# Two units' scores in one interruption, and a bias table whose transfer is issued later

## The chip, the cores and the metric

The kernel runs on one NeuronCore of a Trainium2 chip. The metric is the device time of one execution in microseconds (us). Its engines are TensorE (PE in the profile, with PEld for its weight loads), VectorE (DVE), ScalarE (ACT), GpSimd (POOL) and SyncE (SP), which only issues transfers here. Each engine works through its own instructions in order; semaphores tie the engines together.

## The reference, cut to what matters

One layer of a streaming encoder: 256 rows of a new stream and 64 rows of a running one, 320 columns in all once they are transposed. The input is normalised and projected by one matrix into queries, keys, values and the two halves of a gated branch; attention over a band of chunks, with a relative-position bias and a sink for each head, runs beside that gated branch; both are projected back, and a feed-forward block follows.

```
def sink_attention(q, k, v, bias, sinks, valid=None):
    s = jnp.einsum('...qhgd,...khd->...hgqk', q, k).astype(jnp.float32) * (HEAD_DIM ** -0.5) + bias
    ...
    m = jnp.maximum(jnp.max(s, axis=-1), sink)
    p = jnp.exp(s - m[..., None])
    w = p / (jnp.sum(p, axis=-1, keepdims=True) + jnp.exp(sink - m)[..., None])
    return jnp.einsum('...hgqk,...khd->...qhgd', w.astype(v.dtype), v)

def reference(...):
    q, k, v, zs = project(xp, ln_mix_g[l], w_in[l], q_norm_g[l], k_norm_g[l])
    a_o = attn_prompt(q, k, v, rel_bias_table, attn_sinks[l])
    u, sv = sgu_inputs(zs, sgu_norm_g[l])
    s_o = sgu_prompt(u, sv, sgu_w[l], sgu_b[l])
    ...
    xp = finish(xp, a_o, s_o, out_norm_attn_g[l], out_norm_sgu_g[l], w_out[l],
                ln_ffn_g[l], w_ffn_up[l], w_ffn_down[l])
```

`rel_bias_table` has 32 buckets for each of 16 heads; the bias of a head depends only on the distance between query and key, so one row of 255 values per head holds it all.

## The kernel before, in words

Everything is held transposed, features on the 128 partitions and the 320 rows of both streams along the free axis. Each product is made of three: activations and weights are split into a high part (ScalarE, L116 for weights, L212 for x) and the rest (VectorE, L117 and L213), and TensorE multiplies high by high, high by low and low by high into the same accumulator.

**The first products.** x comes in tiles of 128 features (`xT`, 16 of them; two at a time from the ninth on). As each tile lands, the loop of L223 to L252 splits it, splits the matching rows of the weights for the first quarter of the queries (`q0_ps`) and for keys and values (`kv_ps`), and multiplies. Sums of squares of x are gathered beside it (L295, L297, L299).

**The stream of weights.** After that, `products` (L123) works through the rest of W_in in column groups of 256: q1, q2, q3, then four groups of v and four of u. Each group is four pieces; a piece is one load of 512 KB (`w_raw`), its two halves, and 24 products. `load` (L106) puts these loads on SyncE's queue, each behind the one before it, and takes up to four further transfers from the list `between` along with each: first the cached values, then the 16 reads of the bias (L280), then other constants. So SyncE's queue is weights, then up to four of the list, then weights.

**Interruptions.** With `between_pieces`, small work is put behind a given piece: the mean of the squares of x behind the first piece of q1 (L193, L194, on operands from L180 and L181), key norms, transposes of the values, and the attention by `attend`. TensorE's order is thus written out by hand; `issue_after` places an instruction behind another. The remaining order on the engines comes from a scheduler.

**Attention.** There are eight units: for each of the two key/value heads, query blocks 0 and 1 together, then 2, 3 and 4. `attend(i)` does, in one interruption, the transposes of the probabilities of unit i-2, the scores of unit i (L438) into the two score banks, and the weighted sums of unit i-3 (L520); behind these stands the softmax of unit i on VectorE, ScalarE and GpSimd. The transposes go to a pair of `misc` banks (there are two of these), the scores to `score_bank` (one for each half). attend(0) stands behind the second piece of q3, attend(1) behind its fourth; from the first v group on there are two per group.

**The bias.** GpSimd issues the transfer of the table (L86, `tab`, 16 x 32 values, transposed on the way) while the first tiles of x are loading. After the eighth tile in the program's order it builds the row of 255 values for each head by 29 copies from `tab` (L250) and writes it to DRAM, repeated 15 times (`b_dram`, L252). The 16 reads of `between` fetch it back from there in shifted rows, so that each partition has its own distances (`bias`), and the softmax adds it (L460).

Of the kernel before, what the change touches and what calls it, by code (L numbers as in the profile page):

```python
# [31 lines left out]
def hymba_step_kernel(ctx: ExitStack, tc: tile.TileContext, i, o):  # L32
    nc = tc.nc
# [12 lines left out]
    def misc():  # L46
        return ps_m.tile([P, 512], F32, name="misc", tag="misc")
# [7 lines left out]
    def blk(name, shape, dt=F32):  # L55
        return actp.tile(shape, dt, name=name, tag="B", bufs=6)
# [3 lines left out]
    xT = const.tile([P, KT, T], F32, name="xT")  # L60
# [5 lines left out]
    tab = const.tile([16, 32], F32, name="tab")  # L66
# [16 lines left out]
    for _ in range(4):  # L83
        nc.tensor.matmul(out=warm_ps[:, 0:256], lhsT=nc.const_aps.tensor(0.0, [P, P], F32),
                         rhs=nc.const_aps.tensor(0.0, [P, 256], F32), start=True, stop=True)
    nc.gpsimd.dma_start(out=tab, in_=i["table"].rearrange("b h -> h b"))  # L86
    inv_1k = const.tile([P, 1], F32, name="inv_1k")
    nc.vector.memset(inv_1k, 1.0 / 1024)

# [14 lines left out]
    firsts, loads, between, rests, steps, narrow, carry = [], [], [], [], [], [], []  # L104

    def load(out, in_):  # L106


        for o_, i_ in [(out, in_)] + [between.pop(0) for _ in range(min(4, len(between)))]:
            with tc.issue_after(loads[-1].ins) if loads else nullcontext():  # L110
                loads.append(nc.sync.dma_start(out=o_, in_=i_))  # L111
# [111 lines left out]
    for a, n in [(a, 1) for a in range(8)] + [(a, 2) for a in range(8, KT, 2)]:  # L223
        if a and a % 4 == 0:
            ahead = blk("w_first", [P, 2, 4, 256])
        raw = ahead[:, :, a % 4:a % 4 + n]
        load(xT[:, a:a + n], xv[:, a:a + n])
        for k in range(n if a > 1 else 0):
            load(raw[:, :, k], wv[:, a + k, 0:2048].rearrange("p (j c) -> p j c", j=2)[:, :, 0:256])
        for k in range(a, a + n):  # L230
            split(xT[:, k], g_mix[:, k:k + 1], XH[:, k], XL[:, k], pinned=True)
        hi, lo = [t.rearrange("p (j k) c -> p j k c", j=2)[:, :, 0:n] for t in w_tiles()]
        if a > 1:
            high, low = halves(raw, hi, lo, pinned=True)
        else:
            for j in range(2):
                if a or not j:
                    load(raw[:, j, 0], wv[:, a, j * 1024:j * 1024 + 256])
                high, low = halves(raw[:, j, 0], hi[:, j, 0], lo[:, j, 0], pinned=True)

        for x, (w_, r_) in enumerate(((hi, xh), (hi, xl), (lo, xh))):
            for j, k, g in [(j, k, g) for j in range(2) for k in range(n) for g in range(2)]:
                ps = q0_ps[g] if j == 0 else kv_ps[:, g]
                mm = nc.tensor.matmul(out=ps[:, 0:T], lhsT=w_[:, j, k, g * P:(g + 1) * P], rhs=r_(a + k),  # L244
                                      start=(a + k == 0 and x == 0), stop=(a + k == KT - 1 and x == 2))
        steps.append((high, low, mm.ins))
        if a == 7:
            b_row = sm.tile([16, 255], F32, name="b_row", tag="w1", bufs=3)
            for b, m, n in bucket_runs():
                nc.gpsimd.tensor_copy(out=b_row[:, m:m + n], in_=tab[:, b:b + 1].to_broadcast([16, n]))  # L250
            b_dram = dram.tile([16, 15, 255], F32, name="b_dram")
            nc.gpsimd.dma_start(out=b_dram, in_=b_row[:, None, :].to_broadcast([16, 15, 255]))  # L252
# [133 lines left out]
    def keys():  # L386
        for dst, c in ((kn[:, 0:256], slice(0, 256)), (kn[:, 384:448], slice(256, 320))):
            nc.vector.scalar_tensor_tensor(out=dst, in0=zk[:, c], scalar=g_k, in1=rk[:, c], op0=ALU.mult, op1=ALU.mult)
        for h in range(2):
# [10 lines left out]
                    between_pieces={0: first_norms, 1: lambda: (values(), norm_q(0, (q0_sq, q1_sq[0])), values_out()), 2: keys},  # L400
                    halves_behind={1: lambda: (q0_out, *parts_k[2:4])})
    q2_sq = evict_q(2, q2_ps)
# [18 lines left out]
            yield (w, n0, kv) + blocks[b]  # L421
            n0 += len(blocks[b][4])

    probs, ready, maxed = {}, [], []
    room = blk("vnat", [P, 2560])
    vnat = room[:, 0:2048].rearrange("p (t c) -> p t c", t=2)

# [4 lines left out]
    def scores(u, s_ps):  # L432
        for w, n0, kv, q0, k0, nk, _, _ in parts(u):
            for j in range(2):
                a = 2 * (2 * kv + j)
                for x, p in [(x, p) for x in range(2) for p in range(2)]:
                    hs = slice(p * HD, (p + 1) * HD)
                    mm = nc.tensor.matmul(out=s_ps[p][x * HD:(x + 1) * HD, n0 * P + j * nk:n0 * P + (j + 1) * nk],  # L438
                                          lhsT=qT[hs, q0 // HD, a + x], rhs=kz[hs, kv, k0:k0 + nk], start=True, stop=True)
        return mm  # L440
# [45 lines left out]
    def attend(i, beside=None):  # L486

        n = len(groups)
        turns = [t for t in ((i - 2,), (n - 2, n - 1), ())[max(0, i - n + 1)] if t >= 0]
        outputs = [v for v in ((i - 3,), (i - 3,), (n - 2, n - 1))[max(0, i - n + 1)] if v >= 0]  # L490
        pairs = [[misc(), misc()]] if turns else []
        if i < n or len(turns) > 1 or beside:
            pairs.append([score_bank(p) for p in range(2)])
        s_ps = pairs[-1] if i < n else None
        places = [(pairs[0], 384), (pairs[-1], 384) if len(pairs) > 1 else (pairs[0], 256)]
        hs = [slice(r * HD, (r + 1) * HD) for r in range(2)]

        def behind(mms):
            with tc.issue_after(narrow[-1]):
                narrow.append([mm() for mm in mms][-1].ins)  # L500

        def turn(t, bank):
            s = probs.pop(t)
            behind([lambda p=p, n=n, x=x: nc.tensor.transpose(  # L504
                        out=bank[x][:, (p * 3 + n) * HD:(p * 3 + n + 1) * HD],
                        in_=s[hs[x], p, n].rearrange("x j k -> x (j k)"), identity=ident[hs[x], hs[x]])
                    for p in range(2) for n in range(3) for x in range(2)])

        for t, bank in zip(turns, pairs):
            turn(t, bank)  # L510
        if s_ps:
            behind([lambda: scores(i, s_ps)])
        if beside:
            with tc.issue_after(narrow[-1]):
                outs = beside(pairs[0])
        sides = [(v, [b[:, c:c + P] for b in bank]) + part
                 for (v, part), (bank, c) in zip(((v, part) for v in outputs for part in parts(v)), places)]
        if sides:
            behind([lambda v=v, side=side, n0=n0, n=n, x=x, kv=kv, ts=ts, j=j, p=p:
                    nc.tensor.matmul(out=side[j][hs[p]], lhsT=vz[hs[j], x, kv], rhs=pts[v % 2][hs[j], :, p, n0 + n],  # L520
                                     start=n == 0, stop=n == len(ts) - 1)
                    for v, side, _, n0, kv, _, _, _, _, ts in sides for n, x in enumerate(ts) for j in range(2) for p in range(2)])
        if s_ps:
            softmax(i, s_ps)
        for _, side, _, _, kv, q0, *_ in sides:
            for j in range(2):
                nc.scalar.activation(out=ao[:, 4 * kv + 2 * j:4 * kv + 2 * j + 2, q0:q0 + 64],
                                     in_=side[j].rearrange("p (a q) -> p a q", a=2), func=AF.Copy)
        for t, bank in zip(turns, pairs):
            for x in range(2):  # L530
                with tc.issue_after(maxed[0]) if t and s_ps else nullcontext():
                    nc.vector.tensor_copy(out=pts[t % 2][:, x],
                                          in_=bank[x][:, 0:384].rearrange("k (p n q) -> k p n q", p=2, n=3))

        if beside:
            for out in outs:
                out()

    q3_ps = product(w_in, 0, KT, 768, xh, xl,
                    between_pieces={1: lambda: attend(0), 3: lambda: attend(1)})  # L540
    q3_sq = evict_q(3, q3_ps)

    def add_square(acc, src, first):
        if first:
# [22 lines left out]
    gvs = room[:, 2048:2560].rearrange("p (a t) -> p a t", a=8)  # L567
    for g in range(4):
        v_ps = product(w_in, 0, KT, 2304 + g * 256, xh, xl, between_pieces={
            1: lambda: (attend(2 * g + 2), norm_q(1, (q2_sq, q3_sq)) if g == 0 else None), 3: lambda: attend(2 * g + 3)} if g < 3 else {  # L570
            2: lambda: attend(8)})
        gelu2(v_ps, gv[:, 2 * g:2 * g + 2], maxed[0])
        for a in range(2 * g, 2 * g + 2):
            add_square(acc_v, gv[:, a], a == 0)
        for a in ((), (), range(6), range(6, 8))[g]:
            for dst, c in ((gv[:, a, 0:256], slice(0, 256)), (gvs[:, a], slice(256, T))):
                with tc.issue_after(ready[0]):
                    nc.gpsimd.tensor_scalar(out=dst, in0=gv[:, a, c], scalar1=g_sv[:, a:a + 1], scalar2=None, op0=ALU.mult)
# [225 lines left out]
```

## Time and profile before

| | us |
|---|---|
| median of 3 runs (1235.59 to 1235.89) | 1235.69 |
| the profiled execution | 1235.83 |
| its span, first to last instruction | 1234.0 |
| TensorE busy in it | 1229.5 |
| VectorE busy | 656.8 |
| ScalarE busy | 492.7 |
| GpSimd busy | 109.9 |

A line of the profile names the kernel's line (L...), the engine, the operation, output <- inputs by tile, the shape and a count. In a timeline the first two numbers are start and length in us; what stands in brackets is the engine's idle time before it and what ended that. `q` behind an engine's name is its queue: an instruction that issues or waits. In a table of windows stand the stretch, its length, busy time and count for each engine, then TensorE's granted clock as a share, the DMA engines' busy share and what they moved in GB/s. fp32 matmuls appear as two instructions each.

### The profile page before, as it was taken

To read this page: it belongs to the slowest core of one execution; us is meant where nothing else is said; L and a number is where in the kernel's file an instruction comes from. 1 tells how busy PE (TensorE), PEld (TensorE's weight loads), DVE (VectorE), ACT (ScalarE), POOL (GpSimd) and SP (SyncE) were. 2 spreads that over 40 slices of the span, in tenths; PEclk is the share of its full clock that TensorE was granted. 3 is DMA by queue.
4 is the path that set the end of the run, shared out by engine and by line. 5 is a ranking of instruction groups with operands and counts; after the bars stand their busy time and mean duration, and the time that the engine had idled before them with its cause. 6 is when DMAs were issued, how large, how long until landed. Compare 5 with 4: busy or idle time off the path is not lost.

```text
span 1234.0 us, 20673 instructions
## 1 busy us (share of the span) xinstructions
PE 1229.5 (100%) x8723; PEld 1222.0 (99%) x8723; DVE 656.8 (53%) x741; ACT 492.7 (40%) x655; POOL 109.9 (9%) x141
## 2 busy tenths in 40 slices
PE   9999999999999999999999999999999999999998
PEld 9999999999999999999999999999999999999998
DVE  7868868877864444344444443444444444444343
ACT  7446565435544433323443233333432234433321
POOL 3144653002200000000000000000000000000000
PEclk9999999999999999999999999999999999999999
DMA  9753456444554444445544444444444454445540
GB/s 284 225 146 107 120 144 190 154 144 147 154 153 146 148 150 154 151 144 150 154 153 145 146 154 153 145 148 152 154 149 145 151 154 149 145 151 164 175 159 32
DMA packets 187917, 188.02 MB, mean 152 GB/s; under 512 B 7600, under 2 KB 187360, under 8 KB 187824
## 3 DMA queue, kind: packets, MB, share of 16 engines
q1 hardware_dynamic: 186528, 185.48, 48.5%
q0 software_dynamic: 864, 0.98, 0.4%
q8 instruction: 68, 1.11, 0.4%
q10 hardware_dynamic: 432, 0.24, 0.1%
q14 instruction: 25, 0.20, 0.0%
HBM read 183.10 MB, written 3.35 MB: 151 GB/s over the span
## 4 chain that ended last, share of the span: by engine, by line
PE 99%; DMA 0%; ACT 0%; SPq 0%; DVE 0%; issue 0%; DVEq 0%
PE acc L144 94%; PE misc L144 1%; PE q_ps L244 1%; PE acc L244 1%; PE s_ps L438 1%; DMA xT<-in_xT 0%; PE misc L504 0%; PE misc L520 0%; PE s_ps L520 0%; PE misc L618 0%; PE g_ps L618 0%; PE misc L334 0%; PE misc L606 0%; SPq L111 0%; PE misc L194 0%; PE misc L193 0%
## 5 line engine op out<-in xcount | busy, mean ns | idle before, releaser
L117 DVE TENSOR_TENSOR w_lo<-w_raw,w_hi 128x1024 fp32r<-128x1024 f32 x332 | 417.2, 1257 | 437.0 <-ACT w_hi L116 427.8
L116 ACT ACTIVATE w_hi<-w_raw 128x1024 fp32r<-128x1024 f32 x332 | 351.8, 1060 | 672.0 <-PE acc L144 646.9
L144 PE MATMUL acc<-H2H,w_lo 128*128 128x320 f32 x1024 | 316.4, 309 | 0.0
L144 PE MATMUL acc<-H2H,w_hi 128*128 128x320 f32 x1024 | 316.4, 309 | 0.0
L144 PE MATMUL acc<-H2L,w_hi 128*128 128x320 f32 x1024 | 316.4, 309 | 0.0
L144 PE MATMUL acc<-FH,w_hi 128*128 128x320 f32 x992 | 306.5, 309 | 0.0
L144 PE MATMUL acc<-FL,w_hi 128*128 128x320 f32 x992 | 306.5, 309 | 0.0
L144 PE MATMUL acc<-FH,w_lo 128*128 128x320 f32 x992 | 306.5, 309 | 0.0
L144 PEld LDWEIGHTS acc<-H2H,w_hi 128*128 128x128 f32 x1024 | 192.2, 188 | 0.0
L144 PEld LDWEIGHTS acc<-H2L,w_hi 128*128 128x128 f32 x1024 | 192.2, 188 | 0.0
L144 PEld LDWEIGHTS acc<-H2H,w_lo 128*128 128x128 f32 x1024 | 192.2, 188 | 0.0
L144 PEld LDWEIGHTS acc<-FH,w_hi 128*128 128x128 f32 x992 | 186.2, 188 | 0.0
L144 PEld LDWEIGHTS acc<-FL,w_hi 128*128 128x128 f32 x992 | 186.2, 188 | 0.0
L144 PEld LDWEIGHTS acc<-FH,w_lo 128*128 128x128 f32 x992 | 186.2, 188 | 0.0
L144 PE MATMUL acc<-XH,w_hi 128*128 128x320 f32 x352 | 110.3, 313 | 0.0
L144 PE MATMUL acc<-XH,w_lo 128*128 128x320 f32 x352 | 108.8, 309 | 0.0
L144 PE MATMUL acc<-XL,w_hi 128*128 128x320 f32 x352 | 108.7, 309 | 0.0
L144 PEld LDWEIGHTS acc<-XH,w_hi 128*128 128x128 f32 x352 | 66.1, 188 | 2.7 <-issue 2.3
L144 PEld LDWEIGHTS acc<-XL,w_hi 128*128 128x128 f32 x352 | 66.1, 188 | 0.0
L144 PEld LDWEIGHTS acc<-XH,w_lo 128*128 128x128 f32 x352 | 66.1, 188 | 0.0
L712 DVE SCALAR_TENSOR_TENSOR tf<-acc,r 128x640 f32<-128x640 f32 x32 | 26.4, 825 | 41.8 <-PE acc L144 41.8
L727 DVE TENSOR_TENSOR xT<-xT,acc 128x640 f32<-128x640 f32 x31 | 25.5, 822 | 41.8 <-PE acc L144 41.8
(216 smaller groups left out, 1039.1 us busy)
## 6 DMA issues: line engine op xcount, KB each, us to landing
w_raw<-in_w_up SPq DMA_DIRECT2D x128, 512.0 KB
w_raw<-in_w_down SPq DMA_DIRECT2D x128, 512.0 KB
w_raw<-in_w_in SPq DMA_DIRECT2D x44, 512.0 KB
w_raw<-in_w_out SPq DMA_DIRECT2D x32, 512.0 KB
w_first<-in_w_in SPq DMA_DIRECT2D x14, 256.0 KB
out_yT<-xT SPq DMA_DIRECT2D x7, 320.0 KB
xT<-in_xT SPq DMA_DIRECT2D x8, 160.0 KB
xT<-in_xT SPq DMA_DIRECT2D x4, 320.0 KB
```

The lines of the kernel that those rows point to most:

```text
L116: return (pin(nc.scalar.activation(out=hi, in_=raw, func=AF.Copy)).ins, pin(nc.vector.tensor_tensor(out=lo, in0=raw, in1=hi.bitcast(F32), ...
L117: pin(nc.vector.tensor_tensor(out=lo, in0=raw, in1=hi.bitcast(F32), op=ALU.subtract)).ins)
L144: mm = nc.tensor.matmul(out=out, lhsT=w_[:, k, g * P:(g + 1) * P], rhs=r_(kk), start=(kk == 0 and x == 0), stop=(kk == nk - 1 and x == 2))
L244: mm = nc.tensor.matmul(out=ps[:, 0:T], lhsT=w_[:, j, k, g * P:(g + 1) * P], rhs=r_(a + k), start=(a + k == 0 and x == 0), stop=(a + k == ...
L438: mm = nc.tensor.matmul(out=s_ps[p][x * HD:(x + 1) * HD, n0 * P + j * nk:n0 * P + (j + 1) * nk], lhsT=qT[hs, q0 // HD, a + x], rhs=kz[hs, ...
L712: nc.vector.scalar_tensor_tensor(out=t, in0=ps[:, :, 0:T], scalar=0.0, in1=r2[:, None, :].to_broadcast([P, 2, T]), op0=ALU.max, op1=ALU.mult)
L727: nc.vector.tensor_tensor(out=xT[:, a, c], in0=xT[:, a, c], in1=p, op=ALU.add)
```

## The change

Two things change. The scores of units 0 and 1 are both computed in attend(0), unit 0 into the score banks as before, unit 1 into the pair of `misc` banks; attend(1) behind the fourth piece of q3 is gone, and the softmax of unit 1 is put ahead of attend(2), behind the low weight half of the second piece of the first v group. And the table's transfer is no longer issued at the start: in the loop over x's tiles, after the third, GpSimd first copies one column of that tile into `tab`, which has it wait for the tile's landing, and then issues the transfer, which overwrites that column.

```diff
@@ -83,7 +83,6 @@
-    nc.gpsimd.dma_start(out=tab, in_=i["table"].rearrange("b h -> h b"))
     inv_1k = const.tile([P, 1], F32, name="inv_1k")
@@ -244,6 +243,9 @@
         steps.append((high, low, mm.ins))
+        if a == 2:
+            nc.gpsimd.tensor_copy(out=tab[:, 0:1], in_=xT[0:16, a, 0:1])
+            nc.gpsimd.dma_start(out=tab, in_=i["table"].rearrange("b h -> h b"))
         if a == 7:
             b_row = sm.tile([16, 255], F32, name="b_row", tag="w1", bufs=3)
@@ -421,7 +423,7 @@
-    probs, ready, maxed = {}, [], []
+    probs, ready, maxed, later = {}, [], [], []
@@ -492,6 +494,8 @@
         s_ps = pairs[-1] if i < n else None
+        if i == 0:
+            pairs.append([misc(), misc()])
@@ -509,7 +513,8 @@
         if s_ps:
-            behind([lambda: scores(i, s_ps)])
+            behind([lambda u=u, banks=banks: scores(u, banks)
+                    for u, banks in (enumerate(pairs) if i == 0 else [(i, s_ps)])])
@@ -522,6 +527,8 @@
         if s_ps:
             softmax(i, s_ps)
+        if i == 0:
+            later.append(pairs[1])
@@ -537,8 +544,12 @@
     q3_ps = product(w_in, 0, KT, 768, xh, xl,
-                    between_pieces={1: lambda: attend(0), 3: lambda: attend(1)})
+                    between_pieces={1: lambda: attend(0)})
     q3_sq = evict_q(3, q3_ps)
+
+    def second_softmax():
+        with tc.issue_after(steps[-1][1]):
+            softmax(1, later[0])
@@ -567,7 +578,7 @@
         v_ps = product(w_in, 0, KT, 2304 + g * 256, xh, xl, between_pieces={
-            1: lambda: (attend(2 * g + 2), norm_q(1, (q2_sq, q3_sq)) if g == 0 else None), 3: lambda: attend(2 * g + 3)} if g < 3 else {
+            1: lambda: (None if g else second_softmax(), attend(2 * g + 2), norm_q(1, (q2_sq, q3_sq)) if g == 0 else None), 3: lambda: attend(2 * g + 3)} if g < 3 else {
             2: lambda: attend(8)})
```

## The prediction

> **What bounds the kernel now.** I read the page's head, then the chain that ended last, then each engine's own timeline in the first 90 us. The head says that TensorE is never idle for long:
>
> ```profile
> span 1234.0 us, 20673 instructions
> ...
> PE 1229.5 (100%) x8723; PEld 1222.0 (99%) x8723; DVE 656.8 (53%) x741; ACT 492.7 (40%) x655; POOL 109.9 (9%) x141
> ```
>
> So only two things can move the time: a stall of TensorE, or work that TensorE no longer does. The chain (start, us, what) shows the places that count here:
>
> ```profile
> 1.65 4.04 DMA xT<-in_xT
> ...
> 37.02 0.15 PE misc L193
> ...
> 51.69 3.52 PE acc L144 x24
> ...
> 70.49 1.10 PE s_ps L438 x27
> ...
> 78.83 0.81 PE s_ps L438 x16
> 79.64 7.24 PE acc L144 x48
> ```
>
> TensorE waits for x's second tile, which is issued at 1.65; soon after, the chain is TensorE's alone to the last product. At 78.83 stands the interruption for the second unit's scores, which the change folds into that at 70.49. At 37.02 TensorE does the row-mean matmuls between the first two pieces of q1; they come back below.
>
> **Part 1, one interruption fewer.** A piece of 24 products takes 3.52 (the row of 51.69), so two take 7.04; behind the interruption the two take 7.24. It costs TensorE 0.81 + 0.20 = 1.01 us. The eight score matmuls (16 instructions) still run, now behind those of unit 0. What they cost inside an interruption:
>
> ```profile
> 96.64 0.81 PE s_ps L438 x16
> ...
> 106.69 0.66 PE misc L520 x24
> ```
>
> Upper end: 0.81, the same shape in the middle of an interruption, so 0.20 is saved. Lower end: L520 runs 24 instructions of 128 columns in 0.66; at four to a group that is 0.11 a group, and four groups of 192 columns are 4 x 0.11 x 1.5 = 0.66, so 0.35 is saved. Nothing tells which is nearer; I take the middle, **-0.28**.
>
> Unit 1's scores will lie in the pair of banks that unit 0's transposes write at the interruption of 86.87, and its softmax must have read them by then. VectorE does those reads now at
>
> ```profile
> 81.10 1.39 DVE L460 SCALAR_TENSOR_TENSOR s_rows<-s_ps,rq,bias 128x192 f32<-128x192 f32 x4
> ```
>
> They end at 82.5, over 4 us ahead. The change puts them behind a low weight half that VectorE makes a piece or more ahead of TensorE, so I cost the move at nothing; TensorE's own products are the cover. With that cover gone (reads only once TensorE stands there) it would cost their 1.39.
>
> **Part 2, the table's transfer is late.** GpSimd's timeline, and the DMA issues (KB, us to landing):
>
> ```profile
> 5.54 7.91 POOL L250 COPY b_row<-tab 16x101 f32<-16x101 f32 x29 [1.51 <-DMA tab<-in_table]
> 13.76 0.60 POOL L252 DMA_DIRECT2D b_dram<-b_row  x1 [0.31 <-POOL b_row L250]
> ...
> 46.14 0.52 POOL L580 MEMSET wsT<- 64x512 f32 x1 [31.78 <-DMA wsT<-in_sgu_wT]
> ```
>
> ```profile
> out_sgu_v<-vnat POOLq DMA_DIRECT2D x2, 128.0 KB, 3.4
> b_dram<-b_row POOLq DMA_DIRECT2D x1, 239.1 KB, 7.7
> ...
> out_kpT<-kvx POOLq DMA_DIRECT2D x1, 64.0 KB, 1.9
> ...
> out_vsT<-kvx POOLq DMA_DIRECT2D x1, 32.0 KB, 4.6
> ...
> tab<-in_table POOLq DMA_DIRECT2D x1, 2.0 KB, 4.1
> ```
>
> What it may win: the table's packets leave the queues while x's second tile is on its way. Products ahead of that tile start in pairs 0.30 apart (5.63, 5.93), so the next pair was due at 6.22 and came at 6.63. The gain lies between 0 (the tile lands no sooner) and 0.41.
>
> ```profile
> 5.63 0.46 PE L244 MATMUL q_ps<-XH,w_lo 128*128 128x320 f32 x2
> 5.93 0.46 PE L244 MATMUL acc<-XH,w_lo 128*128 128x320 f32 x2
> 6.63 0.56 PE L244 MATMUL q_ps<-XH,w_hi 128*128 128x320 f32 x2 [0.25 <-ACT w_hi L116]
> ```
>
> What it delays: behind GpSimd's new waiting copy stand the 29 copies that build the bias row and that row's transfer to DRAM; then nothing until 46.14. The third tile has landed by 6.79, since ScalarE reads it there without an idle:
>
> ```profile
> 6.79 0.55 ACT L212 ACTIVATE XH<-xT,cols 128x320 fp32r<-128x320 f32 x1
> ```
>
> With the 0.31 that GpSimd loses between a copy and a transfer, the issue comes at 7.1. To landing it takes between 4.1 (the same transfer, queues just filling) and 7.7; nearest is a small one into full queues, 4.6 to 4.7. **The table is there at 11.8** instead of 5.54.
>
> The copies then meet a busier VectorE. The windows of the row's tile, GpSimd (busy us, copies) and those of VectorE (busy us, instructions):
>
> ```profile
> 5.54:13.45 7.91, 7.91 (x29) 1.00 1.02 336
> 10.34:12.63 2.29, 2.29 (x6) 1.00 1.06 356
> ```
>
> ```profile
> 5.54:13.45 7.91, 5.83 (x11) 1.00 1.02 336
> 10.34:12.63 2.29, 2.29 (x4) 1.00 1.06 356
> 11.80:13.79 1.99, 1.53 (x4) 1.00 1.05 357
> 13.79:21.29 7.50, 7.50 (x12) 1.00 1.07 316
> 21.29:22.40 1.11, 0.00 (x0) 1.00 1.04 366
> 22.40:29.30 6.90, 6.90 (x11) 1.00 1.01 286
> ```
>
> From 10.34 to 12.63 VectorE runs four instructions back to back, and GpSimd gets through four copies beside the two that overlap the edges: one copy for each VectorE instruction, as long as that takes. The whole stretch fits: 11 copies with 11 instructions, the other 18 in the 2.08 that VectorE is idle, 0.116 each. Now from 11.8. To 13.79 VectorE has three instructions (a fourth begins at the edge) and 0.46 idle: 7 copies. To 21.29, twelve without a gap: 19 in all. Ten are left. The idle 1.11 at 21.29 could take nine, but I expect it to close: ScalarE's split, on which VectorE waits there, needs weights on which SyncE's queue waits too, until 21.17, and the queues carry less while the bias row's own transfer is in them (354, then 267 GB/s), which will now come later.
>
> ```profile
> 15.00:18.00 3.00, 3.00 (x23) 3.00 (x22) 3.00 (x7) 3.00 (x6) 0.00 (x0) 1.00 1.08 354
> 18.00:21.00 3.00, 3.00 (x22) 3.00 (x21) 3.00 (x6) 1.90 (x4) 0.00 (x0) 1.00 1.07 267
> ```
>
> ```profile
> 21.17 0.34 SPq L266 DMA_DIRECT2D sinks<-in_sinks  x1
> ```
>
> Then the ten go with the ten instructions of 22.40 to 29.30 (the eleventh is at the edge), moved up by 1.11: copies done at 28.2, issue at 28.5. To landing: 1.9 (a quarter of the bytes, queues nearly empty) to 7.7 (full queues). SyncE will have stopped feeding the queues, so I go by the 128 KB row, 3.4. **The bias row is in DRAM at 31.9**, against 13.76 + 7.7 = 21.46 before.
>
> [...]
>
> Who waits: SyncE's queue holds weight loads and the reads of that row in one fixed order.
>
> ```profile
> 23.79 1.33 SPq L111 DMA_DIRECT2D bias<-b_dram  x2
> 25.32 0.40 SPq L111 DMA_DIRECT2D w_raw<-in_w_in  x1
> ...
> 38.53 0.38 SPq L111 DMA_DIRECT2D w_raw<-in_w_in  x1
> ```
>
> ```profile
> 31.34 1.06 ACT L116 ACTIVATE w_hi<-w_raw 128x1024 fp32r<-128x1024 f32 x1 [1.80 <-DMA w_raw<-in_w_in]
> ```
>
> ```profile
> 34.97 0.49 DVE L181 TENSOR_TENSOR n_hl<-ssq,n_hl 128x320 fp32r<-128x320 f32 x1 [0.91 <-ACT n_hl L180]
> ...
> 49.08 1.23 DVE L117 TENSOR_TENSOR w_lo<-w_raw,w_hi 128x1024 fp32r<-128x1024 f32 x1 [0.34 <-ACT w_hi L116]
> ```
>
> The first read of the row moves from 23.79 to 32.0, 8.2 later, and the weights behind it from 25.32 to 33.5. Their landing took 6.0 (ScalarE at 31.34) in full queues; half a megabyte at 354 GB/s, 1.5, on top of a small transfer's 1.9 gives the low end, 3.4. I take 4.2: ScalarE splits them at 37.7. VectorE's L181 ends at 35.46, 4.1 after that split begins, because it is queued behind the same weights' low half: now 41.8. TensorE wants L181's result at 37.02, so it stalls 4.8. A second check: the weights issued at 38.53 have their low half at 49.08 + 1.23 = 50.3, and TensorE wants it at its third product of the row at 51.69, some 52.0: 1.7 to spare. SyncE can make up perhaps 1.3 on the way, in waits for earlier loads: 8.2 - 1.3 - 1.7 = 5.2. I take **+5.0**. The early gain of up to 0.41 is lost in this stall, which ends when the weights come, whenever TensorE got there.
>
> **Sum.** The profiled execution took 1235.83 (its span 1234.0 and 1.83 around it), 0.14 above the median 1235.69. 1235.83 + 5.0 - 0.28 = 1240.55; on the median's level 1240.4.
>
> **Rivals.**
>
> (a) Hidden after all, so not slower: VectorE does not hold GpSimd's copies more than before, and they take 7.9 again. The row is then done at 19.7, issued at 20.0, in DRAM at 24.6 (a transfer of 4.6), and SyncE loses 0.9 of the 37.02 - 35.46 = 1.56 that L181 has to spare. The mechanism is this slack, and it decides at a landing near 25.3. The time: 1235.69 - 0.28 - 0.41 = 1235.0. For it: the order on VectorE may change and leave more gaps. Against: twelve instructions without a gap from 13.79. Chance 0.13.
>
> (b) The idle 1.11 at 21.29 stays. Copies done at 22.5, in DRAM at 22.8 + 3.8 = 26.6, SyncE 2.9 late, TensorE stalls 2.9 - 1.6 = 1.3: 1235.69 + 1.3 - 0.28 = 1236.7. Against it: the 267 GB/s. Chance 0.13.
>
> (c) After the stall TensorE comes back at a lower clock. The granted clock is 1.00 in each window above, and TensorE never rests that long in this trace. Were the 3.52 of a piece to double for about half of it, that is 1.8 more: 1242.2. Chance 0.12. [...]
>
> The forecast has 0.60; 0.02 is left for a gain that I do not see.
>
> **How the numbers follow.** A measurement of this kernel can tell about 0.2%, 2.5 us, from no change: slower begins at 1238.2. (a) and (b) lie within; no case comes to -2.5, since the gains end at 0.41 and 0.35. Within the forecast the table may land from 11.2 (7.1 + 4.1) to 14.8 (7.1 + 7.7), and the row's transfer may take 1.9 to 5; that spreads the stall from 2.5 to 8, and a small part falls below the bound. Slower 0.60 x 0.93 + 0.12 = 0.68, same 0.30, faster 0.02. The range has (a) at its foot and a landing 3 us later than mine at its top: 1235.0 to 1243.5. The forecast's own range is 1238.0 to 1243.5.
>
> **What would show it.** Right: GpSimd's copies begin near 12 and take 14 to 18 us in all; the row's transfer is issued near 28; SyncE's first bias read stands near 32; TensorE is idle for some 4 to 5 us at L193 or shortly behind; one group of L438 with 48 instructions, costing 0.2 to 0.35 less than the two. Wrong: copies done by 20, or the bias read issued before 25.3, or TensorE without a gap from 37 to 52.

## The result, and the profile after

The changed kernel takes 1246.53 us (median of six runs, 1245.73 to 1247.31), the kernel before 1235.78 beside it (1235.59 to 1236.01): 1.0087 of its time, 95% interval 1.0076 to 1.0098. The profiled execution took 1246.92 against 1235.83, 11.1 more (the medians differ by 10.75). The forecast was 1240.4 and a range to 1243.5: the sign and the path were right, and the size is more than twice the 4.7 that was said.

The head of the page, and below it the chain of waits of the changed kernel (start, us, what):

```profile
span 1245.1 us, 20671 instructions
...
PE 1231.5 (99%) x8723; PEld 1223.9 (98%) x8723; DVE 657.9 (53%) x741; ACT 493.1 (40%) x655; POOL 120.2 (10%) x142
```

```profile
7.54 6.63 DMA tab<-in_table
...
14.22 18.47 POOL b_row L252 x29
...
32.99 4.19 DMA b_dram<-b_row
...
37.20 0.69 SPq L110
...
38.58 4.27 DMA w_raw<-in_w_in
...
42.96 1.06 ACT w_hi L115
...
44.05 1.22 DVE w_lo L116
45.27 0.41 DVE ssq L301
...
46.08 0.48 ACT n_hl L179
...
46.69 0.60 PE misc L192
47.29 0.47 PE misc L193
47.76 15.11 PE acc L143 x96
...
81.96 0.89 PE s_ps L440 x21
...
83.72 14.28 PE acc L143 x96
```

This is the forecast's path, step for step, and each step late: table, copies, bias row to DRAM, SyncE's first bias read, the weights behind it, their halves, the row means. TensorE stands still from 37.18 until 46.69. The row on GpSimd, SyncE's queue, and TensorE's waits say the same from their side (line numbers are one or two off from those of the kernel before; L192 is its L193):

```profile
14.22 18.46 POOL L252 COPY b_row<-tab 16x101 f32<-16x101 f32 x29 [5.85 <-DMA tab<-in_table]
```

```profile
22.03 1.37 SPq L110 DMA_DIRECT2D kzv<-in_cv  x2
37.20 1.33 SPq L110 DMA_DIRECT2D bias<-b_dram  x2
38.58 0.44 SPq L110 DMA_DIRECT2D w_raw<-in_w_in  x1
```

```profile
36.87 0.31 PE L143 MATMUL acc<-XH,w_lo 128*128 128x320 f32 x1
46.69 0.60 PE L192 MATMUL misc<-n_hl,mean_dm 128*128 128x320 f32 x1 [9.51 <-ACT n_hl L179]
```

SyncE issues nothing between 23.4 and 37.20, and the DMA engines run dry (share 0.00 from 28.70 to 32.68). Then a second loss, in the table of windows (stretch, length, then busy time of PE, PEld, DVE, ACT and POOL, granted clock, DMA share, GB/s):

```profile
36.50:39.70 3.20, 0.68 (x5) 0.41 (x3) 0.00 (x0) 0.00 (x0) 0.00 (x0) 1.00 0.11 29
39.70:46.60 6.90, 0.00 (x0) 0.00 (x0) 1.65 (x3) 1.58 (x3) 0.00 (x0) 0.50 0.78 222
46.60:49.94 3.34, 3.25 (x11) 3.10 (x12) 2.42 (x4) 1.85 (x3) 0.00 (x0) 0.50 0.80 224
49.94:52.00 2.06, 2.06 (x16) 2.06 (x15) 1.34 (x2) 0.69 (x1) 0.00 (x0) 1.00 0.84 256
```

The granted clock is at 0.50 from 39.70 to 49.94. The kernel before has, in its chain of waits,

```profile
37.02 0.15 PE misc L193
37.17 0.15 PE misc L194
37.31 14.08 PE acc L144 x96
```

The row means take 0.60 + 0.47 instead of two times 0.15, and the 96 products behind them 15.11 instead of 14.08: 0.77 + 1.03 = 1.8.

The account of the 11.1: the chain comes to L192 at 46.69, and came to its counterpart L193 at 37.02 (+9.67); the clock adds 1.8; the merged interruption takes 0.35 away (81.96 to 83.72 + 14.28 is 16.04; the same stretch of the kernel before went from 70.49 to the interruption at 86.87, 16.38). The sum is 11.12, and the profiled executions differ by 11.09.

### The profile page after: what moved, and what is told of

The parts are those of the page before. It is cut to its first block, busy times and chain, and to the rows that moved or that the text cites. A ratio compares the mean times of both kernels' runs of the same rounds, so it can differ in the third digit from the quotient of the medians.

```text
span 1245.1 us, 20671 instructions
## 1 busy us (share of the span) xinstructions
PE 1231.5 (99%) x8723; PEld 1223.9 (98%) x8723; DVE 657.9 (53%) x741; ACT 493.1 (40%) x655; POOL 120.2 (10%) x142
## 3 DMA queue, kind: packets, MB, share of 16 engines
q8 instruction: 68, 1.11, 0.4%
## 4 chain that ended last, share of the span: by engine, by line
PE 96%; DMA 2%; POOL 1%; SPq 0%; DVE 0%; issue 0%; ACT 0%; DVEq 0%; ACTq 0%
PE acc L143 93%; POOL b_row L252 1%; PE misc L143 1%; DMA tab<-in_table 1%; PE s_ps L440 0%; DMA w_raw<-in_w_in 0%; DMA b_dram<-b_row 0%; DMA xT<-in_xT 0%; PE misc L508 0%; SPq L110 0%; PE misc L525 0%; PE s_ps L525 0%; PE misc L629 0%; PE g_ps L629 0%; PE misc L336 0%
```

## The experiments

**The attend part alone.**

```diff
+    nc.gpsimd.dma_start(out=tab, in_=i["table"]...)        # where it was
-        if a == 2:
-            nc.gpsimd.tensor_copy(out=tab[:, 0:1], in_=xT[0:16, a, 0:1])
-            nc.gpsimd.dma_start(out=tab, in_=i["table"]...)
```

> The changed kernel with the table's transfer put back where it was, at the start, so only the merged interruption is left. Theory (the lateness of the bias row is all of the loss): the stall at the row means is gone, the first bias read stands near 23.8 us again, and the merging saves 0.2 to 0.35 us: 1235.4. Rival (a part of the loss is the merging itself, through later reads of unit 1's scores or a longer interruption): 1236 or more, with an idle of TensorE at or behind the scores of L440's kind.

It took 1235.64 against 1235.89 (ratio 0.9997, 0.9989 to 1.0006): no difference that can be measured, and 0.25 lower, as the saving should be. Its chain of waits has, for the scores and the products behind them,

```profile
70.53 0.89 PE s_ps L438 x21
...
72.28 14.28 PE acc L144 x96
86.56 0.52 PE misc L506 x12
```

70.53 to 86.56 is 16.03, so the merging saves 0.35, and TensorE waits for nothing behind it: the move of unit 1's softmax is free.

**The table part alone.**

```diff
-                    between_pieces={1: lambda: attend(0)})
+                    between_pieces={1: lambda: attend(0), 3: lambda: attend(1)})
```

with the softmax of unit 1 and its scores where they were: the diff is against the changed kernel, and against the kernel before only the table's transfer has moved.

> The kernel before with only the table's transfer moved behind x's third tile; the scores of the second unit keep their own interruption. Theory: the whole loss and no saving, 11.1 us above the kernel before, 1246.9, with the stall at the row means and the granted clock at 0.50 behind it. Rival (the two parts work together): less than 1245.

1245.71 (1243.43 to 1246.96, four runs), 1.0074 of the kernel before (1.0058 to 1.0089). The whole loss is here. The 0.35 more that it should show does not: its runs spread over 3.5 us, ten times that (its profiled execution is taken apart in the last section).

**SyncE's order.** The changed kernel with the reads of the bias row behind q1's weights on SyncE:

```diff
-                between.append((bias[hh * HD:(hh + 1) * HD, p, j], src))
+                behind_q1.append((bias[hh * HD:(hh + 1) * HD, p, j], src))
...
+    between.extend(first_q2 + behind_q1)      # after q1's loads
```

`first_q2` holds the loads of constants that stood behind those reads (`sgb`, `wsT`, `wsd`); they move along.

> The changed kernel, but SyncE issues the 16 reads of the bias row (and the three loads that stood between them and q1's weights) behind all of q1's weight loads, beside those of q2 and q3. Nothing of the table's path is changed: copies from 14 to 33 us and the row in DRAM at 37 as in the changed kernel. Theory (the loss goes only through SyncE's fixed order, weights queued behind the first bias read): no stall at the row means, granted clock 1.00 throughout, and 1235.4, as for the merging alone, if the bias tiles still land before unit 0's softmax reads them (near 80 us); up to 2 us more if they do not. Rival (the late copies hurt by themselves, on VectorE or in the queues): the stall stays in part, 1238 to 1246.

1235.71 (ratio 1.0000, 0.9992 to 1.0009). GpSimd's part is even later than in the changed kernel, and no weight waits for it:

```profile
13.83 20.79 POOL L252 COPY b_row<-tab 16x101 f32<-16x101 f32 x29 [5.61 <-DMA tab<-in_table]
```

```profile
23.74 9.42 SPq L110 DMA_DIRECT2D w_raw<-in_w_in  x4
...
43.75 2.60 SPq L110 DMA_DIRECT2D bias<-b_dram  x4
```

So the lateness of the row costs nothing by itself; SyncE's fixed order turns it into the stall. (The profiled execution of this kernel, 1238.0, was the longest of its eleven, and its TensorE has new waits behind the row means, the longest 0.7 for `kzv`; the median does not show them.)

**What holds the copies.** 28 of the 29 copies as fills, behind the one that stays; the bias is then left out but for the first run of the row (diff shortened):

```diff
-                nc.gpsimd.tensor_copy(out=b_row[:, m:m + n], in_=tab[:, b:b + 1].to_broadcast([16, n]))
+                nc.gpsimd.memset(b_row[:, m:m + n], 0.0)     # for all but the first run
```

> The changed kernel with 28 of the 29 copies that build the bias row replaced by fills with zero of the same shapes, in the same place of GpSimd's order: only the first run of the row holds the table's values, so the bias added to the scores is left out almost wholly. The table still lands at 14.2 us. Theory (a copy reads SBUF and is held as long as VectorE's instructions run back to back): fills read nothing and are not held; 28 x 0.12 = 3.4 us behind the first copy, done near 18.5, the row in DRAM at 22.5 to 26, a stall of 0 to 1.3 us: 1235.5 to 1236.8. Rival (GpSimd itself, or the landing at 14.2, sets the loss): fills take 15 us or more as the copies did, and the time is 1243 or more.

1235.89, the time of the kernel before (1.0002, 0.9993 to 1.0011), with the table there as late as in the changed kernel:

```profile
13.78 0.80 POOL L253 COPY b_row<-tab 16x101 f32<-16x101 f32 x1 [5.02 <-DMA tab<-in_table]
14.53 1.08 POOL L256 MEMSET b_row<- 16x27 f32 x28
15.91 0.59 POOL L258 DMA_DIRECT2D b_dram<-b_row  x1 [0.31 <-POOL b_row L256]
```

28 fills take 1.08 us in the stretch in which the copies took 18.5. A copy by itself is longer than a fill (1.08 / 28 is 0.04): below, the last twelve take 1.54, 0.13 each, which makes an estimate of 3.7 for all 29. The other 14.7 or so is the copies' waiting. In the changed kernel the windows of all engines (the copies are GpSimd's count, the last) show beside whom:

```profile
14.22:21.27 7.05, 7.05 (x50) 7.05 (x49) 7.05 (x12) 7.05 (x13) 7.04 (x12) 1.00 1.09 354
21.27:31.14 9.87, 9.87 (x69) 9.87 (x68) 9.87 (x15) 7.38 (x12) 9.87 (x6) 1.00 0.51 152
31.14:32.68 1.54, 1.54 (x13) 1.54 (x12) 0.02 (x1) 0.00 (x0) 1.54 (x13) 1.00 0.00 0
```

While VectorE runs without a gap, 12 copies go with 12 instructions; then only five (the counts have the one at the edge too) with some 14; and when VectorE has run out of work at 31.14, the last twelve go in 1.54. It is neither ScalarE nor the DMA engines that hold them: both are idle (0.00) from 28.70 on, before VectorE is, and GpSimd stays in one copy until VectorE has done.

```profile
28.70:31.14 2.44, 2.44 (x18) 2.44 (x17) 2.44 (x3) 0.00 (x0) 2.44 (x1) 1.00 0.00 0
```

That copy, alone on GpSimd's timeline, stood through five of VectorE's instructions:

```profile
26.86 4.33 POOL L252 COPY b_row<-tab 16x1 f32<-16x1 f32 x1
```

So the copies, which read `tab`, are held and take 18.5, and the fills, which read nothing, take 1.08 in the same place of GpSimd's order; what makes a copy wait where a fill does not is not shown. Nor does a copy stand through several of VectorE's instructions in every execution: in the second profile of the changed kernel, below, the 29 went in 17.4 us beside 25 VectorE instructions and some 0.5 us of VectorE's idle time, so nearly one for each. Why the executions differ is not shown.

**The table earlier or later.** The same wait put behind x's first or fifth tile (the changed kernel: its third), beside the changed kernel itself, run again:

```diff
-        if a == 2:
+        if a == 0:      # and, in the other kernel, a == 4
```

> The changed kernel itself, unaltered, timed beside the next three on one chip, since its runs spread over 1.6 us. Both theories: 1246.5, between 1245 and 1247.5, TensorE idle 9 to 10 us ahead of L192 and at half clock for some 3.3 us after.

> The changed kernel with the table's transfer behind x's first tile (landed near 3.3 us) instead of the third. Theory: issue near 4, table there at 8 to 10 (4.1 to 6 us), ahead of the stretch in which VectorE runs without a gap, so the copies still find gaps and end near 18 to 21, or at 22.4 in VectorE's next idle; the row is in DRAM by 23 to 27 and the stall is 0 to 1.5: 1235.5 to 1237. Rival (any wait of GpSimd on x costs the whole stall): 1243 or more.

> The changed kernel with the table's transfer behind x's fifth tile, some 3 us later. Theory (the copies end when VectorE first goes idle for long, near 31.2 us, however many are left by then, at 0.12 each): the end moves by at most 1 us and the time is 1246.5 to 1247.5. Rival (the prediction's step, each microsecond that the table lands later is a microsecond of stall): 1249 to 1250.

The changed kernel took 1245.89 (1245.43 to 1246.99; 1.0081, 1.0068 to 1.0095). Behind the first tile it is 1236.77 (1.0009, 1.0000 to 1.0018), behind the fifth 1246.36 (1.0084, 1.0068 to 1.0099). The copies of the three, in that order:

```profile
13.45 17.40 POOL L252 COPY b_row<-tab 16x101 f32<-16x101 f32 x29 [4.72 <-DMA tab<-in_table]
```

```profile
9.00 14.75 POOL L252 COPY b_row<-tab 16x101 f32<-16x101 f32 x29 [4.48 <-DMA tab<-in_table]
```

```profile
16.73 16.36 POOL L252 COPY b_row<-tab 16x101 f32<-16x101 f32 x29 [5.22 <-DMA tab<-in_table]
```

A table 3.3 us later moves the copies' end by 2.2, from 30.85 to 33.09: more than the 1 us of my expectation, less than the rival's 3.3. When VectorE rests, at 31.45, thirteen copies are left and go in 1.65. SyncE's first bias read moves by as much (35.37 to 37.62), but L192 only from 44.28 to 44.70. The scheduler has ordered this kernel otherwise: VectorE's last sum of squares (L301) stands ahead of the late weights' low half (at 30.96) and not behind it (42.78), so the row means no longer wait for that half. The medians are 0.5 apart, the two profiled executions 1.96 (1245.43, the shortest of its four runs, and 1247.39, the longest). So the time of this kernel does not price a later table by itself. A table 4.5 us earlier ends 7.1 us earlier, at 23.75. My expectations for the copies' end, 22.4 at the latest, and for the row's landing in DRAM, 23 to 27, were still short: the row got there at 28.3. Yet L192 stood only 0.65 later than before, and 0.54 of that the products ahead of it already had: the weights, issued at 29.74, landed in 3.9 us.

**The clock behind the stall.** 22 matmuls of zeros where TensorE stands still:

```diff
+        for _ in range(22):          # zeros, fill: a constant tile and a misc bank (shortened)
+            mm = nc.tensor.matmul(out=fill[:, 0:256], lhsT=zeros, rhs=zeros, start=True, stop=True)
+        with tc.issue_after(mm.ins):
             rstd(parts_x[0:2], mean_dm, EPS, rx)
```

> The changed kernel with 22 more matmuls of zeros (128x256, read by nobody, about 0.43 us each at full clock, 9.4 us in all) put on TensorE ahead of the row-mean matmuls, where it stalls. They bring nothing forward: what TensorE waits for comes when it came. Theory (the stall also costs a slower clock after it, 1.8 us): the granted clock stays 1.00 through 52 us and the time is 1.8 less than the changed kernel's, 1244.7; up to 1 less of that gain where the fillers outlast the stall. Rival (the products after the stall are slow for another reason, late weights or the queues): the products stand as far apart as before and the time is the changed kernel's, 1246.5.

1246.15 (1245.59 to 1246.86) against the changed kernel's 1245.89: nothing gained. Yet the clock did what the theory said; of the same windows as above, the second:

```profile
39.70:46.60 6.90, 6.90 (x34) 6.03 (x33) 2.12 (x3) 2.50 (x4) 0.00 (x0) 1.00 0.79 243
```

The row means start at 46.23, since the fillers outlast the stall by half a microsecond (L192's operand is ready at 45.62). From there to the second row means it is 14.57 us instead of 16.18 (46.23 to 60.80; 46.69 to 62.87 in the changed kernel's first profile): the clock's 1.6 is gained. From these to the same transposes (99.21; 99.33) it is 38.41 instead of 36.46, and the gain is lost. Of this 1.95, TensorE's list of waits (us in total, times, longest) has 1.1 that the changed kernel has not:

```profile
PE misc L336 <- DVE kzv L547: 0.7, 1, 0.7
PE acc L143 <- DVE w_lo L116: 0.4, 1, 0.4
```

The merged scores, which take 2.11 here instead of 1.76, are 0.35 more. A part goes through another order on VectorE. Its step behind the row means, L196, stands at 48.67 in the changed kernel; with the fillers the scheduler has it behind one more low weight half:

```profile
48.67 0.48 DVE L196 TENSOR_SCALAR n_xt<-misc 128x320 f32<-128x320 f32 x1
```

```profile
51.54 0.48 DVE L196 TENSOR_SCALAR n_xt<-misc 128x320 f32<-128x320 f32 x1
```

The chain of waits of this run goes from there through VectorE and ScalarE to the `w_lo` that TensorE waits for at 61.99. The wait for `kzv` is no mark of the stall: it is 0.6 and 0.7 with the table behind the first tile and with SyncE's other order, where there is no stall. My expectation left new waits out, and failed there. That VectorE and ScalarE come out of the stall with a backlog, which a slow TensorE would hide, is possible but not shown.

## Why the prediction was wrong in size, point by point

The step that failed is the size of the stall, 5.0 in the sum and 9.7 measured: the table's landing, the copies and the row's transfer were each too short, by 2.4, 2.1 and 0.8. And the clock behind the stall, 1.8, was left out of the sum.

**The path held.** GpSimd's copies behind the table, SyncE's queue behind the row, the weights behind the first read, the row means' operand behind the weights' low half: each is in the chain, and moving only SyncE's reads away, or only making the copies cheap, removes the loss.

**"The table is there at 11.8": 14.2.** The issue was 0.4 late (7.54 for 7.1), and the transfer took 6.6 where I took 4.7 out of 4.1 to 7.7. I went by a small transfer of a later stage; the queues here were full with x and the first weights (share 1.06, 310 GB/s, from 7.54 to 14.22). The rows above have GpSimd wait 4.48 to 5.85 us for it, behind 0.84 for the issue: 5.3 to 6.7, whichever tile it is put behind.

**"One copy for each VectorE instruction": too good by 2.1 us.** I took 16.4 us for the copies; they took 18.5, and 17.4 in the second profile, where the rule nearly held. My reading that VectorE's idle 1.11 at 21.29 would close was right, so rival (b) fell, but from there, in the first profile, five copies went with some fourteen instructions, not one with each. I had made a rule of one short row, four copies beside four instructions.

**"To landing 3.4": 4.2.** The row's transfer took 4.19 in queues that SyncE had left empty (58 GB/s from 32.99 to 37.18, and the row's own 239.1 KB make 57), inside my bounds. With 0.4, 1.9, 2.1 and 0.8 the first bias read came 5.2 late, 37.20 for 32.0.

**From there on right.** Weights to landing 4.27 (4.2 forecast); L181's counterpart ends 4.1 behind the start of the split (46.58 + 0.49 on VectorE's timeline, against 42.96; 4.1 forecast). But the instruction that TensorE waited for is the one before it, L180 (L179 after the change) on ScalarE, so L192 began 3.7 behind that start. So the stall was 9.7 instead of 4.8, by what came in from above.

**The clock was rival (c).** It was in the text at 1.8, with a chance of 0.12. No run had shown the doubling in it: the kernel before has the clock at 1.00 throughout. Behind the stall of the changed kernel the clock is 0.50 until 49.94 and its products stand 0.26 apart, where they stood 0.15 apart ahead of it; that measured 1.8 in the profiled execution, and a clock of 0.50 came in every profile in which TensorE stood still for seven us or more (9.5, 7.3, 7.3 and 7.5). The mistake was to hold it apart as a rival: no row spoke against it for a stall of 4.8 us, so it belonged into the sum with the stall, at least by half. In the profiles of the last section it came 2.4 to 3.5 us after TensorE's last product.

**The range.** Landing, copies and the row's transfer each had bounds of their own, but a later table also meets more of the stretch in which VectorE never rests (14.22 to 31.14 in the changed kernel). They went wrong together, and at the top I had let only the landing move. The upper ends that the text gives (14.8, 3.0 later; a transfer of 5, 1.6 longer) add up to 4.6, taken one for one, a stall of 9.6 and not the 8 that stands there; with the clock that is 1240.4 + 4.6 + 1.8 = 1246.8, and the top of the range stood at 1243.5.

**The small terms.** -0.28 was 0.35, my upper bound: the scores of unit 1 cost 0.66 instead of 0.81, as the row of L520 said. The early gain did not come, for another reason than mine: x's second tile landed earlier (ScalarE reads it at 5.12), but TensorE was not ready for it. On its timeline the first pairs stand 0.70 apart, and the second tile's pair comes at 6.80, where before it came at 6.63:

```profile
4.43 0.90 PE L243 MATMUL q_ps<-XH,w_hi 128*128 128x320 f32 x2
5.13 0.66 PE L243 MATMUL q_ps<-XL,w_hi 128*128 128x320 f32 x2
...
6.80 0.46 PE L243 MATMUL q_ps<-XH,w_hi 128*128 128x320 f32 x2
```

The attend part alone, with the table's transfer at the start, has the same slow first pairs (0.69 apart), so they do not come from the table; their cause stays open.

## What to carry to other kernels

A transfer that is moved is priced at its last reader's place in every queue it passes, and the queue of a third engine, with weights behind a read that waits, can make more of it: here the table's readers began 8.7 us later (14.22 for 5.54), and SyncE's first bias read, with the weights behind it, came 13.4 later (37.20 for 23.79). GpSimd's copies had no fixed price here: 29 took 7.91 where VectorE had 2.08 of rest, 14.75 to 20.79 behind a later table, and in the changed kernel the last twelve went only when VectorE rested, at 31.14. With the table behind x's first tile (1236.77), or with 28 fills for copies (1235.89), the loss was all but gone or gone. Put the clock into the sum for a stall of TensorE as long as those here (7.3 to 9.5 us; 1.8 to 3.2 more), and widen a range by errors that come together.

## What the runs showed of the hardware that was not expected

TensorE's return did not end the slow stretch of its clock. Windows of 0.40 us (columns as above) around both changes, in the changed kernel, in its second profile, and in the table part alone:

```profile
39.60:40.00 0.40, 0.00 (x0) 0.00 (x0) 0.00 (x0) 0.00 (x0) 0.00 (x0) 0.62 0.58 86
49.80:50.20 0.40, 0.40 (x4) 0.40 (x3) 0.00 (x0) 0.40 (x1) 0.00 (x0) 0.83 0.99 305
```

```profile
39.20:39.60 0.40, 0.00 (x0) 0.00 (x0) 0.00 (x0) 0.00 (x0) 0.00 (x0) 0.66 1.04 368
49.40:49.80 0.40, 0.40 (x4) 0.40 (x4) 0.36 (x2) 0.00 (x0) 0.00 (x0) 0.79 0.42 80
```

```profile
40.80:41.20 0.40, 0.00 (x0) 0.00 (x0) 0.00 (x0) 0.00 (x0) 0.00 (x0) 0.87 0.35 94
51.00:51.40 0.40, 0.40 (x3) 0.40 (x2) 0.36 (x2) 0.00 (x0) 0.00 (x0) 0.58 1.22 322
```

In these profiles the windows on the two sides of each of the six show 1.00 and 0.50. Taken as made of these two alone, a share of 0.62 is full clock for 0.10 of the 0.40 us and half clock for the rest, and so on, which makes estimates: the clock falls at 39.70, 39.33 and 41.10 and is back at 49.94, 49.57 and 51.34. It falls 2.5, 2.4 and 3.5 us after TensorE's last product ends, and is halved for 10.24 us each time, although TensorE was back at 46.69, 44.28 and 44.98. The row means and the 96 products behind them take 17.11 in the second profile and 17.59 in the table part alone, against 14.38 before. With that the account closes there too: L192 comes 7.26 and 7.96 later; 7.26 + 2.73 - 0.35 = 9.64 (the profiled executions differ by 9.60) and 7.96 + 3.21 = 11.17 (11.13). So a stall that ended 2.4 us sooner (the second profile) saved only 1.5 in the time (1245.43 for 1246.92): it ran 5.3 us at half clock instead of 3.25. That may be part of why the kernels with the stall spread more from run to run; no run here isolates it. What sets the 10.24 is not shown. Whether filling a stall gains where the order on VectorE stays as it was, was not tried and stays open.
